# Latent attention scores with 288 rows of contraction as two full matmuls and one of 32 rows, the 32-row ones for four blocks on four row sets of the array

## The chip, the cores and the metric

The kernel runs on 1 core of one Trainium2 chip. The metric is the device time in microseconds (us). The kernel before takes 2636.1 us, the median of 3 runs (2635.48 to 2636.65).

## The reference

One layer of a transformer trunk over 1024 latent tokens and 256 context tokens, D = 1024: a SwiGLU half step, two attention branches side by side (2-D neighbourhood attention, "NA", and multi-head latent attention, "MLA"), a gated merge, and a second SwiGLU half step. The change lies in the MLA scores. Cut to that:

```python
def _mla_k(k_nope, k_rope):                 # 64 own dims of a head, 32 rope dims shared by all heads
    return jnp.concatenate([k_nope, broadcast(k_rope)], axis=-1)

def _attend(q, k, v):                       # 8 heads, q 96 wide, keys: 256 context + 1024 latent
    s = jnp.einsum('bqhd,bkhd->bhqk', q * q.shape[-1] ** -0.5, k)
    p = jax.nn.softmax(s, axis=-1)
    return jnp.einsum('bhqk,bkhd->bqhd', p, v)
```

## The kernel before

Every float32 operand of a product is held as a high and a low part, and a product is made of three matmuls: high by high, high by low, low by high (`mm3`). For a score the contraction is 96 rows (64 own, 32 rope), so three matmuls of 96 rows stand for 288 rows of contraction, each with 32 rows of the array empty.

The attention stage runs 64 items: 32 of NA, then 32 of MLA. An MLA item is one head and 256 queries (two sets s of 128). `MlaItem.scores` makes, for each s, two score blocks of 512 latent keys (e = 0, 1) and one of 256 context keys, each in a PSUM bank; `copy_max` (L1639, VectorE) copies a block to SBUF and leaves its row maximum; L1771 (VectorE) reduces these to one maximum per row; L1775 (ScalarE) takes the exponentials, two long ones of 1024 keys and two short ones of 256, in the order long, short, long, short of the program. `MlaItem.values` works in five parts p0 to p4 of 256 keys: four transposes on TensorE into a bank of pool "m", a high part cast out of it on ScalarE (L1801), a low part by a subtraction on VectorE (L1802), and two parts later four 256-column matmuls on these (`w` below). `head_out` (L1611 to L1620) ends an item: one 64-row copy on ScalarE (L1615) in one item, three (L1611, L1612, L1615) in the next, and an addition on VectorE (L1616); every second item has two more transposes (L156, rope). "One-copy" and "three-copy" items alternate.

The main loop runs the scores of item n+3 beside the values of item n: before, a fifth of the scores (one `yield`) goes behind the transposes of each part. TensorE keeps its order as written. The other engines' operations in these functions are placed by a scheduler; each engine runs its own in order. PSUM has 3 banks of pool "s", 3 of "m", 2 of "v", each pool used in turn. The latent-token and context parts of q, k and v come from DRAM scratch by DMAs that one queue (SP) issues; `MlaHead` issues 14 of them for a head, when the first item of that head is started. Tiles of pool "w" (16) hold them, 6 for a head.

Of the kernel before, what the change touches and what calls it, by code (L numbers as in the profile page):

```python
# [9 lines left out]
F32R = mybir.dt.float32r  # L10
# [5 lines left out]
P = 128  # L16
# [3 lines left out]
NLAT = 1024  # L20
NCTX = 256
# [3 lines left out]
QK = 96  # L25
# [13 lines left out]
def f32(ap):  # L39
    return ap.bitcast(F32)  # L40
# [3 lines left out]
def hybrid_block(ctx: ExitStack, tc: tile.TileContext, a: dict, out: bass.AP):  # L44
# [22 lines left out]
    def U(dt=F32, key="u"):  # L67
        return pools[key].tile([P, 1024], dt, tag="u", name=nm("x" + key))
# [4 lines left out]
    def W(dt=F32R):  # L73
        return pools["w"].tile([P, 1024], dt, tag="w", name=nm("w"))
# [13 lines left out]
    def PB(tag):  # L88
        return ps.tile([P, 512], F32, tag=tag, name=nm("b" + tag), bufs=PBUFS[tag])
# [22 lines left out]
    class Engine:  # L112


        def __init__(self, e):
            self.e = e
# [5 lines left out]
    def ld(dst, src):  # L122
        for x in [x for x in waiting if x[1].tensor.name == src.tensor.name]:
            waiting.remove(x)
            put(*x[1:])
        return put(dst, src)
# [23 lines left out]
    vec, act, pool = Engine(nc.vector), Engine(nc.scalar), Engine(nc.gpsimd)  # L150

    def mmul(o, s, m, start, stop):
        return pin(nc.tensor.matmul(o, s, m, start=start, stop=stop, skip_group_check=open_group[0]))  # L153
# [4 lines left out]
    def mm3(o, s, m, start, stop):  # L158
        mmul(o, s[0], m[0], start=start, stop=False)
        mmul(o, s[0], m[1], start=False, stop=False)  # L160
        mmul(o, s[1], m[0], start=False, stop=stop)
# [182 lines left out]
    cols = {}  # L344
# [618 lines left out]
    o = len(plan.main)  # L963
# [7 lines left out]
    e = len(plan.main)  # L971
# [50 lines left out]
    o = len(plan.main)  # L1022
# [6 lines left out]
    for i, d in enumerate(downs):  # L1029
        last = i == len(downs) - 1  # L1030
        o = len(plan.main)
# [535 lines left out]
    o = va_at  # L1567
# [70 lines left out]
    def copy_max(dst, src, m):  # L1638
        nc.vector.tensor_scalar(dst, src, 1.0, FMIN, op0=ALU.mult, op1=ALU.max, accum_out=m)  # L1639
# [90 lines left out]
            return [local, context, edge]  # L1730

    class MlaHead:
        def __init__(self, h):
            self.h = h
            self.qh, self.ql, self.kh, self.kl, self.v, self.kvc = [W() for _ in range(6)]
            b, i = (h % 2) * 64, (h % 4) * 32
            for s, x in enumerate((self.qh, self.ql)):
                ld(f32(x[0:64, :]), qns[h // 2][s, b:b + 64, :])
                ld(f32(x[64:QK, :]), qrs[h // 4][s, i:i + 32, :])
                ld(f32(self.kvc[0:64, s * 256:(s + 1) * 256]), kns[h // 2][s, b:b + 64, NLAT:])  # L1740
                ld(f32(self.kvc[64:QK, s * 256:(s + 1) * 256]), krs[s, :, NLAT:])
            for s, x in enumerate((self.kh, self.kl)):
                ld(f32(x[0:64, :]), kns[h // 2][s, b:b + 64, :NLAT])
                ld(f32(x[64:QK, :]), krs[s, :, :NLAT])
            vsv = vs[:, h * P:(h + 1) * P].rearrange("(t p) c -> p t c", p=P)
            ld(f32(self.v).rearrange("p (t c) -> p t c", t=8), vsv[:, 0:8, :])
            ld(f32(self.kvc[:, 512:768]).rearrange("p (t c) -> p t c", t=2), vsv[:, 8:10, :])

    class MlaItem:
# [2 lines left out]

        def scores(self):
            hd, b = self.head, self.b
            cx = PB("s")
            m, n_, l, r = ST(8), ST(2), ST(4), sums_of(self.n)
            self.prl, self.prc = prl, prc = [U(), U()], T2()
            qq = [[x[:QK, b * 256 + s * P:b * 256 + (s + 1) * P] for x in (hd.qh, hd.ql)] for s in range(2)]
            for s in range(2):
                mm3(cx[:, s * 256:(s + 1) * 256], qq[s], [hd.kvc[:QK, 0:256], hd.kvc[:QK, 256:512]], True, True)  # L1760
            for s in range(2):
                copy_max(prc[:, s * 256:(s + 1) * 256], cx[:, s * 256:(s + 1) * 256], m[:, 3 * s + 2:3 * s + 3])
            yield
            for s in range(2):
                for e in range(2):
                    lat = PB("s")
                    mm3(lat, qq[s], [x[:QK, e * 512:(e + 1) * 512] for x in (hd.kh, hd.kl)], True, True)
                    copy_max(prl[s][:, e * 512:(e + 1) * 512], lat, m[:, 3 * s + e:3 * s + e + 1])
                    if s + e < 2:
                        yield  # L1770
            nc.vector.tensor_reduce(n_, m[:, 0:6].rearrange("p (s c) -> p s c", s=2), axis=AX.X, op=ALU.max, negate=True)  # L1771

            def exp(x, i):
                s = i % 2
                nc.scalar.activation(x, x, AF.Exp, bias=n_[:, s:s + 1], accum_out=l[:, i:i + 1])  # L1775

            def total():
                nc.vector.tensor_tensor(r, l[:, 0:2], l[:, 2:4], op=ALU.add)
                nc.vector.reciprocal(r, r)
                if self.n % 2:  # L1780
                    widen(self.n)

            for s in range(2):
                soft.append(lambda s=s: exp(prl[s], s))
                soft.append(lambda s=s: exp(prc[:, s * 256:(s + 1) * 256], 2 + s))
            soft.append(total)
            yield
# [411 lines left out]
```

## Time and profile before

| What | Value |
|---|---|
| Median of 3 runs | 2636.1 us |
| Profiled execution, its own time / span | 2633.94 us / 2632.2 us |
| TensorE (PE) busy | 2602.1 us, 99% |
| TensorE weight loads (PEld) busy | 2215.3 us, 84% |
| VectorE (DVE) busy | 1854.2 us, 70% |
| ScalarE (ACT) busy | 1151.8 us, 44% |
| Chain that ended last | PE 56%, issue 32%, DVE 5%, ACT 5% |
| Granted TensorE clock | 0.999 of full speed |

The shares are means over stages with different limits. A busy TensorE is not TensorE at its peak: matmuls are pipelined, so the records of neighbours overlap, and what a matmul costs is the distance from its start to the next one's start. The MLA items lie between about 1495 and 1770 us. In the rows below, "[1.18 <-DVE st L1771]" means that the engine sat idle for 1.18 us before the instruction and that VectorE's line 1771 ended it.

### The profile page before, as it was taken

To read this page: it belongs to the slowest core of one execution; us is meant where nothing else is said; L and a number is where in the kernel's file an instruction comes from. 1 tells how busy PE (TensorE), PEld (TensorE's weight loads), DVE (VectorE), ACT (ScalarE), POOL (GpSimd) and SP (SyncE) were. 2 spreads that over 40 slices of the span, in tenths; PEclk is the share of its full clock that TensorE was granted. 3 is DMA by queue.
4 is the path that set the end of the run, shared out by engine and by line. 5 is a ranking of instruction groups with operands and counts; after the bars stand their busy time and mean duration, and the time that the engine had idled before them with its cause. 6 is when DMAs were issued, how large, how long until landed. Compare 5 with 4: busy or idle time off the path is not lost.

```text
span 2632.2 us, 37730 instructions
## 1 busy us (share of the span) xinstructions
PE 2602.1 (99%) x13728; PEld 2215.3 (84%) x13728; DVE 1854.2 (70%) x3478; ACT 1151.8 (44%) x2193; POOL 220.3 (8%) x368
## 2 busy tenths in 40 slices
PE   8999999999999999999999999999999999999998
PEld 6888888888888788889889999987888888888887
DVE  4778876588776676864569988877436777565876
ACT  6622223522223753433439887772365222234111
POOL 1000000000000400001004422220020000000001
PEclk9999999999999999999999999999999999999999
DMA  8544433444433665745977723217244433225333
GB/s 303 166 157 145 150 106 125 157 160 161 163 130 99 229 227 188 247 150 181 304 285 281 211 75 75 67 49 230 86 148 166 138 120 109 76 92 193 120 96 128
DMA packets 196218, 414.14 MB, mean 157 GB/s; under 512 B 24960, under 2 KB 66112, under 8 KB 196032
## 3 DMA queue, kind: packets, MB, share of 16 engines
q1 hardware_dynamic: 196032, 411.73, 47.3%
q8 instruction: 108, 1.77, 0.3%
q14 instruction: 78, 0.64, 0.1%
HBM read 308.30 MB, written 103.35 MB: 156 GB/s over the span
## 4 chain that ended last, share of the span: by engine, by line
PE 56%; issue 32%; DVE 5%; ACT 5%; DMA 1%; POOL 1%; SPq 0%; DVEq 0%; POOLq 0%; ACTq 0%
PE bs L153 23%; PE bm L153 17%; PE bv L153 13%; PE bm L156 2%; ACT xu L1775 1%; DVE xu L1639 1%; DVE t L1802 1%; ACT t L1801 1%; DVE xv L120 1%; PE bs L156 1%; POOL st L120 1%; ACT t L120 1%; DVE t L120 1%; DVE xu L120 1%; ACT t L1775 0%
## 5 line engine op out<-in xcount | busy, mean ns | idle before, releaser
L153 PE MATMUL bm<-xu,xu 128*128 128x512 f32 (+2 forms) x2376 | 569.4, 388 | 0.9 <-ACT t L120 0.6
L153 PEld LDWEIGHTS bm<-xu,xu 128*128 128x128 f32 x2376 | 437.5, 188 | 89.9 <-ACT t L120 1.9
L153 PE MATMUL bs<-xu,xu 128*128 128x512 f32 (+1 forms) x1800 | 433.5, 385 | 0.0
L153 PEld LDWEIGHTS bs<-xu,xu 128*128 128x128 f32 x1800 | 332.3, 188 | 67.4 <-issue 0.8
L153 PE MATMUL bs<-xv,xu 128*128 128x512 f32 x1488 | 357.3, 389 | 0.3 <-DVE t L120 0.3
L153 PE MATMUL bv<-xv,xu 128*128 128x512 f32 x1342 | 335.4, 389 | 0.0
L153 PEld LDWEIGHTS bs<-xv,xu 128*128 128x128 f32 x1488 | 279.2, 188 | 58.6 <-issue 0.7
L120 ACT CAST xu<-t 128x512 fp32r<-128x512 f32 x260 | 158.2, 616 | 355.8 <-DVE t L120 354.6
L153 PEld LDWEIGHTS bv<-xv,xu 128*128 128x128 f32 x1342 | 251.9, 188 | 52.3
L120 DVE TENSOR_TENSOR xu<-t,xu 128x512 fp32r<-128x512 f32 x260 | 178.5, 688 | 127.2 <-ACT xu L120 127.2
L120 DVE TENSOR_TENSOR xu<-xv,xu 128x512 fp32r<-128x512 f32 (+2 forms) x244 | 182.3, 767 | 57.1 <-ACT xu L120 54.0
L153 PE MATMUL bs<-w,w 96*128 96x512 f32 (+3 forms) x832 | 206.2, 366 | 2.5 <-DVE st L1664 2.2
L120 POOL TENSOR_SCALAR st<-st 128x1 f32<-128x1 f32 (+1 forms) x66 | 34.6, 524 | 1977.8 <-ACT t L120 1959.4
L120 DVE TENSOR_TENSOR xu<-xu,xu 128x512 fp32r<-128x512 f32 (+1 forms) x218 | 151.0, 698 | 67.1 <-ACT xu L120 66.7
L120 ACT CAST xu<-xv 128x512 fp32r<-128x512 f32 (+2 forms) x216 | 136.8, 692 | 125.9 <-DVE xv L120 60.3
L153 PE MATMUL bm<-t,xu 128*128 128x256 f32 (+1 forms) x1272 | 165.3, 287 | 0.6 <-ACT t L120 0.4
L153 PEld LDWEIGHTS bm<-t,xu 128*128 128x128 f32 x1272 | 160.7, 191 | 6.0 <-ACT t L120 0.8
L153 PE MATMUL bv<-xu,xu 128*128 128x512 f32 x602 | 161.7, 389 | 0.0
L120 ACT ACTIVATE t<-t 128x512 f32<-128x512 f32 (+1 forms) x94 | 57.3, 609 | 221.6 <-DVE t L120 212.6
L153 PE MATMUL bv<-t,w 128*128 128x256 f32 x896 | 151.5, 288 | 2.7 <-DVE t L1802 2.0
L153 PEld LDWEIGHTS bv<-t,w 128*128 128x128 f32 x896 | 132.8, 189 | 18.5 <-DVE t L1802 6.8
L120 ACT CAST xu<-xu 128x512 fp32r<-128x512 f32 (+1 forms) x218 | 134.2, 627 | 15.8 <-DMA xu<-in_f1w 8.1
(216 smaller groups left out, 3679.2 us busy)
## 6 DMA issues: line engine op xcount, KB each, us to landing
d<-t SPq DMA_DIRECT2D x272, 256.0 KB, 2.8
xv<-d SPq DMA_DIRECT2D x68, 512.0 KB, 4.5
xv<-in_f1w SPq DMA_DIRECT2D x64, 512.0 KB, 3.6
xu<-in_f1w SPq DMA_DIRECT2D x61, 512.0 KB, 3.8
xu<-in_f2w SPq DMA_DIRECT2D x60, 512.0 KB, 3.8
t<-in_wada SPq DMA_DIRECT2D x112, 256.0 KB, 3.9
t<-d SPq DMA_DIRECT2D x76, 256.0 KB, 3.3
xu<-in_winT SPq DMA_DIRECT2D x38, 512.0 KB, 4.6
```

What stands on the lines that cost most here:

```text
L120: return lambda *x, **y: pin(f(*x, **y))
L153: return pin(nc.tensor.matmul(o, s, m, start=start, stop=stop, skip_group_check=open_group[0]))
L156: return pin(nc.tensor.transpose(o, x, i))
L1639: nc.vector.tensor_scalar(dst, src, 1.0, FMIN, op0=ALU.mult, op1=ALU.max, accum_out=m)
L1775: nc.scalar.activation(x, x, AF.Exp, bias=n_[:, s:s + 1], accum_out=l[:, i:i + 1])
L1801: nc.scalar.copy(t[0], pb)
L1802: nc.vector.tensor_tensor(t[1], pb, f32(t[0]), op=ALU.subtract)
```

## The change

The 288 rows of contraction are laid out anew. `q1` (128 rows) holds q high (64), rope high (32) and rope low (32); `k1` holds k high (64), rope high (32) and rope high again. `q2` holds q high and q low; `k2` holds k low and k high. So two matmuls of 128 rows do 256 of the 288 rows. What is left, rope high of q by rope low of k, has 32 rows. `q3` and `k3` hold these for the four latent blocks on four sets of 32 partitions, and four 32-row matmuls, one for each block and each on its own rows of the array, open the four blocks' banks together at the head of an item. For the context block the third product is a 128-row matmul against `c3`, zero but for 32 rows.

The latent blocks now come first in an item and the context block last; of the four latent banks the first comes from pool "m" and three from "s", and the context bank from "m". `MlaHead` issues 21 loads for a head, and 5 once for a tile of pool "y" that all heads share (`k3`, `c3`), which two memsets on GpSimd clear in part. A head takes 7 tiles of pool "w".

```diff
     class MlaHead:
+        shared = None
         def __init__(self, h):
-            self.qh, self.ql, self.kh, self.kl, self.v, self.kvc = [W() for _ in range(6)]
+            self.q1, self.q2, self.q3, self.k1, self.k2, self.v, self.kvc = [W() for _ in range(7)]
             b, i = (h % 2) * 64, (h % 4) * 32
-            for s, x in enumerate((self.qh, self.ql)):
-                ld(f32(x[0:64, :]), qns[h // 2][s, b:b + 64, :])
-                ld(f32(x[64:QK, :]), qrs[h // 4][s, i:i + 32, :])
-                ld(f32(self.kvc[0:64, s * 256:(s + 1) * 256]), kns[h // 2][s, b:b + 64, NLAT:])
-                ld(f32(self.kvc[64:QK, s * 256:(s + 1) * 256]), krs[s, :, NLAT:])
-            for s, x in enumerate((self.kh, self.kl)):
-                ld(f32(x[0:64, :]), kns[h // 2][s, b:b + 64, :NLAT])
-                ld(f32(x[64:QK, :]), krs[s, :, :NLAT])
+            if MlaHead.shared is None:
+                x = MlaHead.shared = U(F32R, "y")
+                for p in ((0, 64), (96, P)):
+                    pool.memset(f32(x[p[0]:p[1], 512:512 + NCTX]), 0.0)
+                ld(f32(x[64:QK, 512:512 + NCTX]), krs[1, :, NLAT:])
+                for g in range(4):
+                    ld(f32(x[32 * g:32 * g + 32, 0:512]), krs[1, :, (g % 2) * 512:(g % 2) * 512 + 512])
+            self.k3, self.c3 = MlaHead.shared[:, 0:512], MlaHead.shared[:, 512:512 + NCTX]
+            q, r, n = qns[h // 2], qrs[h // 4], kns[h // 2]
+            parts = [(self.q1, [(0, q[0, b:b + 64, :]), (64, r[0, i:i + 32, :]), (QK, r[1, i:i + 32, :])]),
+                     (self.q2, [(s * 64, q[s, b:b + 64, :]) for s in range(2)])]
+            for k, o, c in ((self.kvc, 0, slice(NLAT, NLAT + NCTX)), (self.k1, None, slice(0, NLAT))):
+                one = k[:, 0:NCTX] if o == 0 else k
+                two = k[:, NCTX:2 * NCTX] if o == 0 else self.k2
+                parts += [(one, [(0, n[0, b:b + 64, c]), (64, krs[0, :, c]), (QK, krs[0, :, c])]),
+                          (two, [(64 - s * 64, n[s, b:b + 64, c]) for s in range(2)])]
+            for x, rows in parts:
+                for o, y in rows:
+                    ld(f32(x[o:o + y.shape[0], :]), y)
+            for g in range(4):
+                ld(f32(self.q3[32 * g:32 * g + 32, 0:512]).rearrange("p (b c) -> p b c", b=4),
+                   r[0, i:i + 32, :].rearrange("p (b s c) -> p b s c", b=4, s=2)[:, :, g // 2, :])
...
         def scores(self):
-            cx = PB("s")
...
-            qq = [[x[:QK, b * 256 + s * P:b * 256 + (s + 1) * P] for x in (hd.qh, hd.ql)] for s in range(2)]
+            pairs = [(s, e) for s in range(2) for e in range(2)]
+            lats = [PB("m" if x == 0 else "s") for x in range(4)]
+            for g, lat in enumerate(lats):
+                rows = slice(32 * g, 32 * g + 32)
+                mmul(lat, hd.q3[rows, b * P:(b + 1) * P], hd.k3[rows, :], True, False)
+            cols = [slice(b * 256 + s * P, b * 256 + (s + 1) * P) for s in range(2)]
+            for (s, e), lat in zip(pairs, lats):
+                keys = slice(e * 512, (e + 1) * 512)
+                mmul(lat, hd.q1[:, cols[s]], hd.k1[:, keys], False, False)
+                mmul(lat, hd.q2[:, cols[s]], hd.k2[:, keys], False, True)
+                copy_max(prl[s][:, keys], lat, m[:, 3 * s + e:3 * s + e + 1])
+                yield
+            cx = PB("m")
             for s in range(2):
-                mm3(cx[:, s * 256:(s + 1) * 256], qq[s], [hd.kvc[:QK, 0:256], hd.kvc[:QK, 256:512]], True, True)
+                x = cx[:, s * 256:(s + 1) * 256]
+                mmul(x, hd.q1[:, cols[s]], hd.kvc[:, 0:256], True, False)
+                mmul(x, hd.q2[:, cols[s]], hd.kvc[:, 256:512], False, False)
+                mmul(x, hd.q1[:, cols[s]], hd.c3, False, True)
             for s in range(2):
                 copy_max(prc[:, s * 256:(s + 1) * 256], cx[:, s * 256:(s + 1) * 256], m[:, 3 * s + 2:3 * s + 3])
-            yield
-            for s in range(2):
-                for e in range(2):
-                    lat = PB("s")
-                    mm3(lat, qq[s], [x[:QK, e * 512:(e + 1) * 512] for x in (hd.kh, hd.kl)], True, True)
-                    copy_max(prl[s][:, e * 512:(e + 1) * 512], lat, m[:, 3 * s + e:3 * s + e + 1])
-                    if s + e < 2:
-                        yield
             nc.vector.tensor_reduce(n_, m[:, 0:6].rearrange("p (s c) -> p s c", s=2), axis=AX.X, op=ALU.max, negate=True)
```

The scheduler also places VectorE's and ScalarE's work differently. VectorE before, at the end of a three-copy item (subtractions of p3 and p4, the last score block `xu`, the maximum, then p0 of the next item; `bm` and `bs` are PSUM banks):

```order
L1802 TENSOR_TENSOR t_16074<-bm_16068,t_16073 128x512
L1778 TENSOR_TENSOR st_15767<-st_15887 128x2
L1802 TENSOR_TENSOR t_16093<-bm_16087,t_16092 128x512
L1779 RECIPROCAL st_15767<-st_15767 128x2
L1639 TENSOR_SCALAR xu_16004,st_15999<-bs_16099 128x512
L1771 TENSOR_REDUCE st_16000<-st_15999 128x2
L1802 TENSOR_TENSOR t_16115<-bm_16109,t_16114 128x512
```

VectorE of the change at the same place (L1830 is L1802, L1799 is L1771):

```order
L1830 TENSOR_TENSOR t_17598<-bm_17592,t_17597 128x512
L1806 TENSOR_TENSOR st_17292<-st_17412 128x2
L1830 TENSOR_TENSOR t_17615<-bm_17609,t_17614 128x512
L1807 RECIPROCAL st_17292<-st_17292 128x2
L1639 TENSOR_SCALAR t_17530,st_17524<-bm_17621 128x256 x2
L1830 TENSOR_TENSOR t_17641<-bm_17635,t_17640 128x512
L1799 TENSOR_REDUCE st_17525<-st_17524 128x2
L1639 TENSOR_SCALAR xu_17648,st_17645<-bm_17651 128x512
L1639 TENSOR_SCALAR xu_17648,st_17645<-bs_17652 128x512
```

The two context copies have taken the place of a latent one, and the subtraction of the next p0 now stands ahead of the maximum instead of behind it; two latent copies follow the maximum at once.

ScalarE before, in a three-copy item from its first long exponential on (`128x1024` the long ones, `128x256` the short ones, `t<-bm` the casts of p1 to p4):

```order
L1775 ACTIVATE xu_15888,st_15887<-xu_15888,st_15886 128x1024
L1801 CAST t_16023<-bm_16018 128x512
L1775 ACTIVATE t_15890,st_15887<-t_15890,st_15886 128x256
L1775 ACTIVATE xu_15889,st_15887<-xu_15889,st_15886 128x1024
L1611 COPY t_16037<-bv_15943 64x256
L1612 COPY t_16040<-bv_15943 64x256
L1615 COPY t_16037<-bv_15943 64x256
L1801 CAST t_16053<-bm_16048 128x512
L1775 ACTIVATE t_15890,st_15887<-t_15890,st_15886 128x256
L1801 CAST t_16073<-bm_16068 128x512
L1801 CAST t_16092<-bm_16087 128x512
```

ScalarE of the change at the same place (L1803 is L1775, L1829 is L1801):

```order
L1803 ACTIVATE xu_17413,st_17412<-xu_17413,st_17411 128x1024
L1829 CAST t_17551<-bm_17546 128x512
L1803 ACTIVATE t_17415,st_17412<-t_17415,st_17411 128x256
L1611 COPY t_17563<-bv_17467 64x256
L1612 COPY t_17566<-bv_17467 64x256
L1615 COPY t_17563<-bv_17467 64x256
L1829 CAST t_17579<-bm_17574 128x512
L1803 ACTIVATE xu_17414,st_17412<-xu_17414,st_17411 128x1024
L1829 CAST t_17597<-bm_17592 128x512
L1803 ACTIVATE t_17415,st_17412<-t_17415,st_17411 128x256
L1829 CAST t_17614<-bm_17609 128x512
```

The second long exponential has moved from ahead of the copies to behind the cast of p2, so it stands ahead of the cast of p3.

## Rows read from the trace of the kernel before

**Rows 1.** Stages: start:end us, length, busy us (instructions) by engine, clock, DMA.
```profile
1557.31:1565.95 8.64, 8.59 (x62) 7.78 (x61) 7.06 (x22) 7.09 (x17) 2.26 (x4) 1.00 0.56 136
1524.06:1750.08 226.02, 225.03 (x1599) 207.47 (x1598) 190.89 (x568) 180.20 (x406) 55.74 (x95) 1.00 0.23 58
```

**Rows 2.** Timeline, ScalarE, a three-copy and a one-copy item: start us, duration us, instruction.
```profile
1591.04 1.15 ACT L1775 ACTIVATE xu<-xu,st 128x1024 f32<-128x1024 f32 x1 [1.18 <-DVE st L1771]
...
1592.18 0.56 ACT L1801 CAST t<-bm 128x512 fp32r<-128x512 f32 x1
1592.65 0.51 ACT L1775 ACTIVATE t<-t,st 128x256 f32<-128x256 f32 x1
...
1593.15 1.15 ACT L1775 ACTIVATE xu<-xu,st 128x1024 f32<-128x1024 f32 x1
...
1594.29 0.36 ACT L1611 COPY t<-bv 64x256 f32<-64x256 f32 x1
...
1594.93 0.37 ACT L1615 COPY t<-bv 64x256 f32<-64x256 f32 x1
1595.32 0.59 ACT L1801 CAST t<-bm 128x512 fp32r<-128x512 f32 x1
...
1599.44 1.16 ACT L1775 ACTIVATE xu<-xu,st 128x1024 f32<-128x1024 f32 x1 [1.07 <-DVE st L1771]
...
1602.60 0.19 ACT L1775 ACTIVATION_READ_ACCUMULATOR xu<-xu,st 128x1 f32 x1
1602.82 0.37 ACT L1615 COPY t<-bv 64x256 f32<-64x256 f32 x1
...
1607.67 1.16 ACT L1775 ACTIVATE xu<-xu,st 128x1024 f32<-128x1024 f32 x1 [1.15 <-DVE st L1771]
```

**Rows 3.** Timeline, VectorE, the same three-copy item.
```profile
1591.52 0.41 DVE L1639 TENSOR_SCALAR_CACHE_REDUCE t<-bs 128x256 f32<-128x256 f32 x1
...
1591.86 0.42 DVE L1639 TENSOR_SCALAR_CACHE_REDUCE t<-bs 128x256 f32<-128x256 f32 x1
...
1592.78 0.69 DVE L1802 TENSOR_TENSOR t<-bm,t 128x512 fp32r<-128x512 f32 x1 [0.50 <-ACT t L1801]
1593.39 0.68 DVE L1639 TENSOR_SCALAR_CACHE_REDUCE xu<-bs 128x512 f32<-128x512 f32 x1
...
1595.33 0.41 DVE L1616 TENSOR_TENSOR t<-t,bv 64x256 f32<-64x256 f32 x1 [0.64 <-ACT t L1615]
1595.94 0.69 DVE L1802 TENSOR_TENSOR t<-bm,t 128x512 fp32r<-128x512 f32 x1 [0.20 <-ACT t L1801]
...
1599.25 0.16 DVE L1771 TENSOR_REDUCE st<-st 128x2 f32<-128x6 f32 x1
```

**Rows 4.** Timeline, TensorE, the same item: first start us, us to last end, instructions merged.
```profile
1588.93 0.95 PE L153 MATMUL bs<-w,w 96*128 96x256 f32 x6
1589.72 0.64 PE L153 MATMUL bv<-t,w 128*128 128x256 f32 x4
1590.20 0.60 PE L156 MATMUL bm<-ident,xu 128*128 128x128 f32 x4
1590.55 0.94 PE L153 MATMUL bs<-w,w 96*128 96x512 f32 x3
1591.33 0.64 PE L153 MATMUL bv<-t,w 128*128 128x256 f32 x4
1591.81 0.38 PE L156 MATMUL bv<-ident,rope 128*128 128x128 f32 x2
```

**Rows 5.** Timeline, TensorE, eight 32-column matmuls on four column sets, and what follows.
```profile
1847.42 0.64 PE L153 MATMUL bv<-t,strip 128*32 128x256 f32 x8
1847.99 1.20 PE L153 MATMUL bm<-xo,xu 128*128 128x512 f32 x4
```

**Rows 6.** Timeline, SP: DMA issues for the first two MLA heads, merged.
```profile
1477.45 22.72 SPq L132 DMA_DIRECT2D w<-d  x30
```

**Rows 7.** Timeline, TensorE, the first MLA scores.
```profile
1495.54 0.84 PE L153 MATMUL bs<-w,w 96*128 96x256 f32 x5
```

## The prediction, made before the changed kernel ran

> **What bounds the kernel now.** I read the page first: TensorE is busy 99% of the span and heads the chain that ended last, which says that every matmul taken away is time won. So the second view is the stages, for the MLA items alone: in 226.02 us from 1524 to 1750 TensorE has 225.03 busy, but VectorE 190.89 and ScalarE 180.20 [rows 1]. These are 27 items (a long exponential starts each), 8.37 us an item, of which VectorE has 7.07 to do. The third view is the timelines of one item, engine by engine, and it turns the picture round.
>
> ScalarE waits over a microsecond for VectorE's maximum before the first long exponential of every item (1.18, 1.07, 1.15), and VectorE then waits for ScalarE: for the cast of p1 behind that exponential (0.50), for the copy L1615 (0.64), for the cast of p2 (0.20) [rows 2, 3]. No wait on TensorE stands among VectorE's. Follow a three-copy item from its exponential at 1591.04: long exponential, cast, short, long exponential, three copies, cast of p2 at 1595.32, all end to end on ScalarE; 0.62 later the subtraction of p2 at 1595.94; from there VectorE works without a gap to the maximum at 1599.25, and 0.19 later the next exponential starts, at 1599.44 [rows 2, 3]. That is a closed loop of 8.40 us over two engines, without TensorE. The one-copy item behind it takes 8.23, to 1607.67 [rows 2], so a pair takes 16.63. Every second head has 8.64 in place of 8.40 [rows 1].
>
> What would TensorE alone need? By distances of starts [rows 4]: four transposes 0.35 (1590.20 to 1590.55), three 512-column matmuls 0.78 (to 1591.33), four 256-column ones 0.48 (to 1591.81), the six context matmuls 0.79 (1588.93 to 1589.72). A part with a latent block is 1.61, the one with the context block 1.62: 8.06 an item, and some 0.2 for the two rope transposes in every second one (half of 0.35), so 16.3 a pair against 16.63 measured. TensorE is a close second, busy since its records overlap, and it is the loop that sets the pace.
>
> **The change part by part.**
>
> *TensorE's matmuls.* An item loses twelve 512-column matmuls of 0.26 (a third of 0.78) and gets eight, and four of 32 rows. If these run beside each other they cost about one. No row shows row sets; the nearest one is of column sets: eight 256-column matmuls on four sets, two rounds, take 0.57 from the first start to the next full matmul (1847.42 to 1847.99), where four full ones of that width already take 0.48 [rows 4, 5]. That holds the change to another layout of the array and back. So the four cost from 0.26 (one matmul) through 0.57 (the eight) to 1.04 (four times 0.26, no overlap). I take 0.35, nearer to the packed end. TensorE then needs 0.35 + 0.35 + 0.52 + 0.48 = 1.70 for the first part, 1.35 for each of the next three, 1.62 for the last: 7.37 an item, 0.69 less than 8.06, and 15.0 a pair. Taken at its word that is 32 x 0.69 = 22 us, the gain if TensorE set the pace. In the last part 0.48 and 0.79 are as before: the context block keeps six matmuls.
>
> The Trainium skill (TensorEngine Tiling (Array Packing), Key Properties) says that a change of tiling mode drains TensorE. No row separates such a drain; one lies inside the 0.57 of [rows 5], so the trace neither contradicts it nor prices it. The same page (PSUM Bottleneck) warns that packing speeds TensorE but not the emptying of PSUM; that is this loop, on which the trace decides.
>
> *VectorE and ScalarE.* No operation is added or removed in an item: five casts, five subtractions, four latent copies, two context copies, one maximum, four exponentials. Their places change, as the pieces of order show. Two moves matter. The subtraction of the next p0 now runs ahead of the maximum (0.61 more on the loop there: 1592.78 to 1593.39 [rows 3]) and two latent copies follow the maximum at once, where VectorE used to have a subtraction and two context copies. And the second long exponential stands behind the cast of p2: p2 comes out of ScalarE 1.15 earlier, p3 later.
>
> So I walk the loop again, with the distances of [rows 2, 3]: long exponential to next 1.14, cast to short exponential 0.47, short to next 0.50, first copy to third 0.64, third copy to cast 0.39, cast to subtraction 0.60, L1615 to L1616 0.40, a subtraction or latent copy on VectorE 0.61, a context copy 0.34 (1591.52 to 1591.86), maximum to exponential 0.19. I take 0.07 for each of the small reciprocal and sum.
>
> Three-copy item, exponential at 0. ScalarE: cast p1 1.14, short 1.61, copies from 2.11 to 2.75, cast p2 3.14, long 3.61, cast p3 4.75, short 5.22, cast p4 5.72. VectorE: two copies from -0.11, done at 1.11; subtraction p1 1.74 (waits for its cast); copy 2.35; L1616 3.15 (waits); p2 3.74 (waits); copy 4.35; p3 5.35 (waits); p4 6.32 (waits); sum and reciprocal; context copies 7.07 and 7.41; p0 7.75; maximum 8.36; exponential 8.55.
>
> One-copy item. The copy starts 0.22 behind a readout (1602.60 to 1602.82), here at 2.24; cast p2 2.63, long 3.10, cast p3 4.24, short 4.71, cast p4 5.21. VectorE: p1 1.74; L1616 2.64; p2 3.23; copies 3.84 and 4.45; p3 5.06; p4 5.81 (waits); context copies from 6.56; p0 7.31; maximum 7.92; exponential 8.11.
>
> The pair: 16.66 against 16.63. Waits have moved from one operation to another, and the loop is as long as before. The 8.64 of every second head stays, since ScalarE's copies stand on the path in both walks. Each start in the walk may be off by some 0.1 an item: 16 pairs at 0.03, bounds -3 and +4 us; I take +0.5.
>
> *What is late next.* The first latent bank now comes from pool "m", where three banks pass in turn through seven uses an item. It gets the bank that p4 has just left, so the four 32-row matmuls wait for the subtraction of p4 (6.32 + 0.69 = 7.01 in the three-copy item), and all of TensorE's queue behind them: the four latent blocks, the transposes of p1 and on to the next p0. TensorE needs some 7.4 from there to the end of the next p0's transposes, at 7.01 + 7.4 - 8.55 = 5.9 of the next item; its cast must have started by 6.7 for the subtraction at 7.31. About 0.8 of slack by these rows, less by pipeline tails of 0.2 to 0.4 (a record's 0.94 against 0.78, [rows 4]) after each wait. So TensorE's time won turns into a wait of its own for p4, and costs nothing as long as the 32-row matmuls are packed.
>
> *Loads.* A head takes 21 loads for 14, the first one 26 with the shared tile. SP issued 30 in 22.72 us, 0.76 each, waits for free buffers among them [rows 6]. For later heads SP has an item's time and more to spare: hidden. For the first, 14 x 0.76 ended at 1488, and 26 x 0.76 end at 1497, where the first scores stood at 1495.54 [rows 7]; the 32-row operands come near the end. TensorE may stall once, from 0 to some 5 us with landing; the last three NA items lie ahead and part of it hides there. I take 1. The two memsets lie on GpSimd ahead of these loads: nothing.
>
> *Sum.* The profiled execution has 2633.94 us of its own (span 2632.2): +0.5 + 1 = 2635.4. The runs' median is 2.2 above the profiled one, so I predict 2637.6, rounded to 2637.5.
>
> **The rivals.**
>
> *TensorE sets the pace after all.* For it: 99% busy, and VectorE's 7.07 an item leave room below 8.3. Against: VectorE's waits are all on ScalarE, and the loop closes without TensorE. If the loop gave way fully: 22 us, 2614; half of it, if the new order of the two engines is shorter than my walk: 2625. I name 2624.
>
> *The 32-row matmuls run one after another, or the layout change is dear.* For it: no row of row sets. Against: the column sets of [rows 5]. They cost 1.04, TensorE needs 16.3 a pair again, and now with the wait for p4 in its queue: the 0.8 of slack less tails is gone, and 0.3 to 0.9 a pair come on top, 16 x 0.6 = 10 us: 2646, slower. It decides from about 0.8 us for the four. Behind it stands the Trainium skill (TensorE: Matmul & The Clock Gate, Part 3), which gives 3.07 times for four row tiles: by that the four would cost 0.34 (an estimate: 4 x 0.26 / 3.07), which is the packed case; no run here shows it yet.
>
> *The first loads stall more, and the loop is longer by 0.2 a pair*: 3 + 3 us, 2643.
>
> **How the numbers follow.** The forecast 0.60 (its own range 2632 to 2643), TensorE's pace 0.15, unpacked 0.14, loads and a longer loop 0.11. Within 0.2% is 2630.8 to 2641.4, about what a measurement of this kernel can tell from no change. Faster: 0.13 of the first rival and 0.02 of the forecast, 0.15. Slower: 0.14, most of 0.11 and 0.03 of the forecast, 0.26. Same: 0.59. The range for 8 in 10 leaves out most of the first rival and half of the second: 2629 to 2646.
>
> **What would show it.** Right: an MLA item still 8.2 to 8.4 us from exponential to exponential; ScalarE still waiting for the maximum; TensorE idle some 0.5 an item, in front of the 32-row matmuls with VectorE's L1830 as the releaser; the four of them starting within a few ns of each other. Wrong: items of 7.5 to 8.0 us; or the four starting 0.2 us apart; or TensorE waiting for a DMA at 1495 for more than 3 us.

## The result and the profile after

| | Before | Changed |
|---|---|---|
| Median (lowest to highest), 20 runs of each | 2635.98 us (2633.22 to 2637.91) | 2640.18 us (2637.03 to 2643.34) |
| Ratio to before, 95% interval | | 1.0016 (1.0009 to 1.0022) |
| Span of the profiled execution | 2632.2 us | 2635.3 us |
| TensorE busy in it | 2602.1 us | 2596.0 us |
| 27 steady MLA items | 226.02 us | 226.03 us |

The change is 4 us slower, by the interval 0.09 to 0.22%, which is about the 0.2% that the prediction calls no change. TensorE's saving bought nothing in the steady items, and something was lost elsewhere. The windows of the changed kernel show both (columns as in [rows 1]); the first stretch is the entry, from the transposes ahead of the first MLA scores to the exponential that opens the 27 items.

```profile
1493.50:1526.72 33.22, 29.55 (x204) 25.28 (x203) 27.50 (x90) 23.54 (x56) 11.08 (x20) 1.00 0.76 179
...
1526.72:1752.75 226.03, 219.18 (x1595) 192.90 (x1594) 191.30 (x568) 179.88 (x406) 55.90 (x95) 1.00 0.36 81
```

The same view of the kernel before, for the entry from the same point of the program on:

```profile
1494.60:1524.06 29.46, 29.32 (x206) 26.87 (x205) 26.72 (x89) 23.51 (x55) 10.61 (x18) 1.00 0.50 123
```

The entry is 3.76 us longer with TensorE no busier (29.55 against 29.32): 3.67 us in which it stood idle, against 0.14. The 27 items answer to the second of [rows 1]: as long as before, TensorE busy 5.85 us less, VectorE and ScalarE as before. So nothing was hidden by chance: the saving turned into idle time.

The two spans differ by only 3.1 us, because the changed kernel reaches the entry 1.10 us earlier (1493.50 for 1494.60), in a stretch that the change doesn't touch. From the entry to the end it loses 4.2 us: 3.76 in the entry, 0.01 in the 27 items, some 0.4 behind them. There TensorE waits once for 1.24 us for a cast on ScalarE, until 1764.40 (the longest such wait before is 0.45), and its granted clock is 0.74 from 1764 to 1768.

**A steady item.** ScalarE's timeline, the changed kernel (start, duration, instruction, idle time before it and who ended it):

```profile
1593.68 1.15 ACT L1803 ACTIVATE xu<-xu,st 128x1024 f32<-128x1024 f32 x1 [0.95 <-DVE st L1799]
...
1602.19 1.15 ACT L1803 ACTIVATE xu<-xu,st 128x1024 f32<-128x1024 f32 x1 [0.95 <-DVE st L1799]
...
1610.32 1.15 ACT L1803 ACTIVATE xu<-xu,st 128x1024 f32<-128x1024 f32 x1 [0.97 <-DVE st L1799]
```

These answer to [rows 2]: 8.51 and 8.13 from exponential to exponential, 16.64 a pair, where before had 8.40 and 8.23, 16.63. ScalarE still waits for the maximum (L1799 is L1771). VectorE closes the loop as in [rows 3]:

```profile
1594.80 0.69 DVE L1639 TENSOR_SCALAR_CACHE_REDUCE xu<-bs 128x512 f32<-128x512 f32 x1 [0.55 <-PE bs L153]
...
1600.05 0.69 DVE L1830 TENSOR_TENSOR t<-bm,t 128x512 fp32r<-128x512 f32 x1 [0.22 <-ACT t L1829]
...
1601.40 0.68 DVE L1830 TENSOR_TENSOR t<-bm,t 128x512 fp32r<-128x512 f32 x1
1602.01 0.15 DVE L1799 TENSOR_REDUCE st<-st 128x2 f32<-128x6 f32 x1
```

p4 waits for its cast, then the context copies, p0 and the maximum follow without a gap, and the exponential comes 0.18 behind it. Waits of VectorE for TensorE are new: 0.55 for the second latent block here and 0.28 for the third, 19.4 us in 41 waits over the 27 items, where the same view of the kernel before lists none. They take the place of waits for ScalarE (for casts 10.6 us in place of 22.4, for L1615 1.0 in place of 10.3). They are absorbed: the subtraction of p2 starts when its cast lets it, and the maximum comes 8.33 behind the exponential, where the prediction's walk has 8.36. TensorE in the same item (answering to [rows 4]):

```profile
1600.79 0.49 PE L153 MATMUL bm<-xy,w 32*128 32x512 f32 x1 [0.25 <-DVE t L1830]
1600.80 0.50 PE L153 MATMUL bs<-xy,w 32*128 32x512 f32 x3
```

The four start within 10 ns, so they do run beside each other, and they wait for the subtraction of p4 (L1830), which ends at 1600.74.

**The entry.** TensorE's timeline, the changed kernel:

```profile
1494.06 0.60 PE L156 MATMUL bm<-ident,xu 128*128 128x128 f32 x4
1495.69 0.46 PE L153 MATMUL bm<-xy,w 32*128 32x512 f32 x1 [1.03 <-DVE st L1671]
1495.86 1.17 PE L153 MATMUL bs<-xy,w 32*128 32x512 f32 x3
1496.96 0.73 PE L153 MATMUL bm<-w,w 128*128 128x512 f32 x2
...
1509.38 0.47 PE L153 MATMUL bm<-xy,w 32*128 32x512 f32 x1 [0.86 <-DVE xu L1699]
...
1517.16 0.46 PE L153 MATMUL bm<-xy,w 32*128 32x512 f32 x1 [1.78 <-DVE st L1807]
```

Three stalls, each in front of 32-row matmuls: 1.03, 0.86 and 1.78 us, together the 3.67 us of idle time. The second and third are for a PSUM bank that VectorE has not yet left: the subtraction L1699 that empties it ends at 1509.22 and at 1517.01 (the third names the reciprocal just behind it). The first names an instruction of VectorE, but it is for operands: the four loads of `q3`, issued from 1491.05 to 1492.99, land at 1495.60, 1495.82, 1496.10 and 1496.43, and the four matmuls start one by one just behind, at 1495.69, 1495.86, 1496.19 and 1496.56. From the transposes to the first full matmul 2.90 us pass, 0.97 where nothing waits. The queue, SP's timeline, says why:

```profile
1475.80 0.42 SPq L132 DMA_DIRECT2D xy<-in_bias  x1
1479.08 2.17 SPq L132 DMA_DIRECT2D xy<-d  x5
1481.35 21.07 SPq L132 DMA_DIRECT2D w<-d  x32
```

SP stands 2.9 us before the shared tile's loads (`xy<-d`), whose buffer an NA bias tile still holds, and `q3` comes last of the operands in the loads behind them.

### The profile page after: what moved, and what is told of

It reads as the page before. It is cut to its first block, busy times and chain, and to the rows that moved or that the text cites. A ratio compares the mean times of both kernels' runs of the same rounds, so it can differ in the third digit from the quotient of the medians.

```text
span 2635.3 us, 37805 instructions
## 1 busy us (share of the span) xinstructions
PE 2596.0 (99%) x13728; PEld 2200.2 (83%) x13728; DVE 1854.6 (70%) x3478; ACT 1151.7 (44%) x2193; POOL 220.7 (8%) x370
## 3 DMA queue, kind: packets, MB, share of 16 engines
q8 instruction: 108, 1.77, 0.3%
## 4 chain that ended last, share of the span: by engine, by line
PE 54%; issue 32%; ACT 7%; DVE 5%; POOL 1%; DMA 1%; SPq 0%; DVEq 0%; POOLq 0%; ACTq 0%
PE bs L153 22%; PE bm L153 17%; PE bv L153 12%; ACT xu L1803 2%; ACT t L1829 2%; PE bm L156 2%; DVE xv L120 1%; DVE t L1830 1%; POOL st L120 1%; PE bs L156 1%; ACT t L1803 1%; DVE t L120 1%; DVE xu L120 1%; DVE t L1639 1%; ACT t L120 1%
## 5 line engine op out<-in xcount | busy, mean ns | idle before, releaser
L153 PEld LDWEIGHTS bv<-xu,xu 128*128 128x128 f32 x602 | 112.7, 188 | 23.2
```

## The experiments

My theory, 1: VectorE and ScalarE set the pace of the steady items through the maximum, TensorE's saving becomes waiting, and the 4 us are lost at the entry. The rivals: TensorE sets the pace and the layout change eats its saving; or the loss is spread over all items.

**e_late_before, e_late_after, e_pin_after: is it the loop?** An exponential is issued one item later, so it never waits for a fresh maximum. The same edit is made on both kernels, and ScalarE's instructions of these items are pinned in the order of the program (`pin(...)` around them, not shown). In the changed kernel that is the order that ScalarE has anyway, and the third run, with the pins alone, is the control. In the kernel before it is not: the pins also move the second long exponential from ahead of the copies ([rows 2]) to behind the cast of p2, where the change has it, and no run has the pins alone on that kernel. So the exponentials are not "in the same places" there, as the first expectation has it. VectorE's order is the scheduler's in all three; with late exponentials one latent copy of a three-copy item changes places with the addition L1616.

```diff
+    late = []
...
         soft_n, soft[:] = list(soft), []
+        if n + 2 >= 4 * NH:
+            late.append(soft_n)
+            soft_n = late.pop(0) if len(late) > 1 else []
```

> The kernel before, with the exponentials of an MLA item issued one item later (two items after its scores, still one item ahead of their use), in the same places of ScalarE's order, which is pinned. No exponential waits for a maximum that has just been made. Theory 1 (the loop of VectorE and ScalarE through the maximum sets the pace, 16.63 a pair, and TensorE alone would need 16.3 to 16.4): the wait for the maximum goes, items take 8.15 to 8.2, 3 to 5 us less than before, 2631 to 2633. Rival (TensorE or VectorE's own work sets the pace): no change, 2636.

> The change, with the exponentials of an MLA item issued one item later, as in the run on the kernel before. Theory 1 (the loop hides TensorE's gain): with the loop through the maximum open, TensorE's own need shows, 7.4 to 7.6 us an item, and the way from the cast of p1 over the subtraction of p4 and the 32-row matmuls to the next cast of p1 takes some 7.5; 8 to 20 us less than the change, 2620 to 2632, and far more than the same edit gives the kernel before. Rival 1 (TensorE's saving is eaten by the layout change, TensorE sets the pace): no change, 2640. Rival 2 (VectorE's order alone sets it): as much as the same edit gives the kernel before, about 2636.

> The change with ScalarE's casts, copies and exponentials of the MLA items pinned in the order of the program, and nothing else: the control for the runs with late exponentials, which pin them too. Theory 1 (it is the age of the exponentials, not the pinned order, that opened the loop): as the change, 2639 to 2641, items 8.5 and 8.1 in turn. Rival (the pinned order itself gave the gain): 2630 to 2633.

Measured: 2632.65 us (0.9987, 0.9978 to 0.9996), 2631.48 (0.9986, 0.9977 to 0.9994), and the control 2641.29 (1.0021, 1.0012 to 1.0030), with its 8.51 and 8.12 unchanged. ScalarE in e_late_before, where the pins have moved the second long exponential:

```profile
1595.16 0.59 ACT L1801 CAST t<-bm 128x512 fp32r<-128x512 f32 x1
1595.64 1.15 ACT L1775 ACTIVATE xu<-xu,st 128x1024 f32<-128x1024 f32 x1
```

Windows over the same 27 items; first the kernel before with late exponentials:

```profile
1525.89:1747.58 221.69, 221.69 (x1596) 207.35 (x1595) 197.17 (x568) 181.14 (x408) 55.44 (x94) 1.00 0.24 60
```

then the changed one:

```profile
1525.16:1743.36 218.20, 215.05 (x1594) 192.60 (x1594) 189.96 (x566) 181.64 (x408) 55.77 (x95) 1.00 0.38 85
```

With the loop open the kernel before is held by TensorE: busy 221.69 of 221.69, pairs of 16.41, close to the 16.3 that the prediction adds up from starts. The items had taken 4.3 us more (3.3 by the medians); how much of that is the later exponential and how much the moved one isn't shown. The changed kernel gains 7.8 in the same items, 8.7 by the medians, and there the control leaves only the age of the exponentials and that one exchange on VectorE: theory 1, and both rivals fall. But the gain is at the small end of 8 to 20, since TensorE's own need was wrong. Side by side, with late exponentials in both, the change is 3.5 us shorter in the 27 items but only 1.2 by the medians, within their scatter: at its entry TensorE still waits 1.38, 0.59 and 0.65 us in front of 32-row matmuls.

**e_serial, e_lazy: what do the four 32-row matmuls cost?** All four on row set 0, then each alone in front of its block's pair.

```diff
 e_serial
-                rows = slice(32 * g, 32 * g + 32)
+                rows = slice(0, 32)
...
 e_lazy
+                if apart:
+                    lats[g] = PB("s")
+                    rope_rows(g)
+                lat = lats[g]
                 mmul(lat, hd.q1[:, cols[s]], hd.k1[:, keys], False, False)
```

> The change, but all four 32-row matmuls read rows 0 to 31 (of q3 and k3), so that they follow one another on one row set; two of the four blocks then get another block's keys or queries for their last 32 rows. In the trace of the change the four start within 10 ns and the path from the last transpose to the first full matmul is some 0.6 us longer than without them. Theory 1 (they run beside each other, and TensorE has under 0.5 us an item to spare behind the loop of VectorE and ScalarE): the four start some 0.2 us apart, 0.6 to 0.8 more an item, TensorE needs 8.5 to 8.7 and becomes the bound: 2645 to 2652. Rival (what the four cost is the layout change, not their work, or the records only look parallel): no change, 2640.

> The change, but each of the four 32-row matmuls stands alone, directly in front of the two full matmuls of its block, on its own row set, and all four banks come from pool s. Four changes of the array's layout an item in place of one. Theory 1 (the price of the four, some 0.6 us on TensorE's path, is nearly all the change of layout and back, paid once for four): each costs 0.5 to 0.6, TensorE needs some 9.5 us an item, 1.2 to 1.5 above the loop: 2670 to 2684. Rival (the layout change is free and a 32-row matmul costs what a full one does, 0.24): TensorE needs 8.2, and with the waits for pool m gone at the entry 2636 to 2641.

Measured: 2648.67 us (1.0052, 1.0039 to 1.0066; four runs) and 2683.9 (1.0184, 1.0165 to 1.0202; two runs). In e_serial the 27 items take 235.95 us, 9.9 more than in the change, so it is the steady items that pay. One part of an item on TensorE, from its transposes to the next ones. The kernel before (late exponentials), three matmuls of 96 rows, 1.61:

```profile
1616.79 0.60 PE L156 MATMUL bm<-ident,xu 128*128 128x128 f32 x4
1617.14 0.94 PE L153 MATMUL bs<-w,w 96*128 96x512 f32 x3
...
1618.40 0.60 PE L156 MATMUL bm<-ident,xu 128*128 128x128 f32 x4
```

The change (late exponentials), a part without 32-row matmuls, 1.37, and one with the four, unhindered, 2.01:

```profile
1615.19 0.60 PE L156 MATMUL bm<-ident,xu 128*128 128x128 f32 x4
1615.54 0.70 PE L153 MATMUL bs<-w,w 128*128 128x512 f32 x2
...
1616.56 0.60 PE L156 MATMUL bm<-ident,xu 128*128 128x128 f32 x4
...
1620.95 0.60 PE L156 MATMUL bm<-ident,xu 128*128 128x128 f32 x4
1621.48 0.50 PE L153 MATMUL bm<-xy,w 32*128 32x512 f32 x1
1621.48 0.50 PE L153 MATMUL bs<-xy,w 32*128 32x512 f32 x3
1621.92 0.73 PE L153 MATMUL bm<-w,w 128*128 128x512 f32 x2
...
1622.96 0.38 PE L156 MATMUL bm<-ident,xu 128*128 128x128 f32 x2
```

e_lazy, one 32-row matmul alone, 1.99:

```profile
1600.09 0.60 PE L156 MATMUL bm<-ident,xu 128*128 128x128 f32 x4
1600.62 0.50 PE L153 MATMUL bs<-xy,w 32*128 32x512 f32 x1
1601.04 0.72 PE L153 MATMUL bs<-w,w 128*128 128x512 f32 x2
...
1602.08 0.38 PE L156 MATMUL bm<-ident,xu 128*128 128x128 f32 x2
```

e_serial, four on one row set:

```profile
1600.56 0.49 PE L153 MATMUL bm<-xy,w 32*128 32x512 f32 x1
1600.90 0.85 PE L153 MATMUL bs<-xy,w 32*128 32x512 f32 x3
1601.68 0.73 PE L153 MATMUL bm<-w,w 128*128 128x512 f32 x2
```

A full matmul costs 0.24 (1.61 less 1.37). One 32-row matmul alone costs 0.62 (1.99 less 1.37), four beside each other 0.64, four on one row set 0.68 more (1.12 to the first full matmul for 0.44), 1.32. So some 0.4 (0.62 less 0.24) is the way into the other layout and back, paid once a group. The weight loads, which elsewhere run ahead, show it in the changed kernel (late exponentials):

```profile
1621.48 0.18 PEld L153 LDWEIGHTS bm<-xy,w 32*128 32x128 f32 x1 [0.17 <-DVE st L1806]
...
1621.91 0.30 PEld L153 LDWEIGHTS bm<-w,w 128*128 128x128 f32 x2 [0.24 <-DMA w<-d]
```

0.17 of idle going in, 0.24 coming out; e_lazy has the same 0.17 and 0.25. The releasers named are not the cause, as they differ from group to group. In e_lazy TensorE sets the pace (busy in all 257.61 us of 1531.39 to 1789.00, items of 9.65 and 9.74), and its second and third MLA item do not wait for a bank at the entry. It takes one bank at a time, and all from pool "s", and TensorE is slower in it; which of these spares it the wait isn't shown.

**e_loads, e_entry: the entry.** The four loads of `q3` first and the shared tile late; then the first three MLA items one part later.

```diff
 e_loads
...
+            for g in range(4):
+                ld(f32(self.q3[32 * g:32 * g + 32, 0:512]).rearrange("p (b c) -> p b c", b=4),
...
+            rows_in(first + parts[:2])
             if MlaHead.shared is None:
...
+            rows_in(parts[2:])
...
 e_entry
+            if self.n < 4 * NH + 3:
+                yield
             lats = [PB("m" if x == 0 else "s") for x in range(4)]
```

> The change with the loads of a head in another order: the four of q3 first, then q1, q2, k1 and k2, and only then the shared tile and the context parts, so that the queue no longer waits for the shared tile's buffer ahead of everything. Theory 1 (the four us are lost at the entry into the MLA items, some 2 of them because the 32-row operands come last in the queue): the wait in front of the first four 32-row matmuls, 1.03 us and the spread of the other three, is gone and the time falls by 1.5 to 2, to 2638 to 2639. Rival (the entry loses its time to the banks alone): no change, 2640.

> The change, but the first three MLA items, whose scores run beside NA items of three parts, begin one part later. Their 32-row matmuls then take the bank that the context block has left, in place of the one that the part just before has left. Theory 1 (two stalls of 1.1 and 2.0 us for that bank, and part of a third for the loads): 3 to 4.5 us less than the change, 2635.5 to 2637. Rival (the loss is spread over all the items, as the cost of the layout change or a longer loop): 2639 to 2640.

Measured: 2640.88 us (1.0018, 1.0010 to 1.0027) and 2638.84 (1.0013, 1.0004 to 1.0021). Both gave less than theory 1 asked. TensorE's timeline in e_loads:

```profile
1497.19 0.60 PE L156 MATMUL bm<-ident,xu 128*128 128x128 f32 x4
...
1497.73 0.51 PE L153 MATMUL bs<-xy,w 32*128 32x512 f32 x2
1498.44 0.49 PE L153 MATMUL bs<-xy,w 32*128 32x512 f32 x1 [0.20 <-DVE xu L1639]
1498.86 0.74 PE L153 MATMUL bm<-w,w 128*128 128x512 f32 x2
```

The wait for loads is gone, and behind it a wait of the fourth for an "s" bank appears: a second bank wait that the late loads had covered. 1.2 of 1.9 us are won there (1.67 from transposes to the first full matmul, for 2.90), and lost again in this execution at 1520 (below). The medians show no gain. Sorted by the mean granted clock of a run they hint at one: eight of the eleven runs of e_loads are at 0.997 and take 2640.38 to 2641.34 us, the change's four at 0.997 take 2642.91 to 2643.34. So the loads may be worth some 2 us, spent again where the clock fell more often; that isn't shown. In e_entry stalls of 0.45, 0.52 and 1.12 us are left, of 3.67 before: VectorE leaves other banks late too, once in front of transposes. The intervals of its ratio and of the change's overlap, so its 1.3 us is not shown; that the entry holds the loss is shown by the windows, not by these two.

**v_first3, v_all, v_two, v_two_vec: what can be had.** Late exponentials, the loads of e_loads, and the 32-row matmuls later in the item: in the first three items by one part; in all by one; in all others by two; and the last with VectorE pinned in program order too.

```diff
+            for _ in range(1 if self.n < 4 * NH + 3 else 2):
+                yield
             lats = [PB("m" if x == 0 else "s") for x in range(4)]
```

> The change with the exponentials one item later, the first three MLA items begun one part later, and the loads of a head in the order q3, q1, q2, k1, k2, shared tile, context. The sum of three edits measured alone (8.7, 1.3 and no gain by the medians; in the traces 1.4 of the entry's 3.8 us and 1.1 of the first stall). Theory 1: 2629 to 2630.5, all three beside each other. Rival (the entry's stalls only move, since VectorE is late there): 2631.5, as with the late exponentials alone.

> As the run before it in this list, but every MLA item begins one part later, behind the transposes of p1, so that its first latent bank is the one that the context block has left and not the one of p4. With the loop open the trace of the change shows items of 8.0 to 8.25 where TensorE's own start distances add to 7.8 and 7.9 with rope: 0.2 to 0.4 a pair is the wait of the 32-row matmuls on the subtraction of p4. Theory 1: this wait goes, pairs of 15.8 to 15.9 in place of 16.1 to 16.25: 4 to 6 us less than the run before it, 2624 to 2626. Rival (VectorE's own chain sets these items, or the wait comes back on the context block's bank): no gain, 2629 to 2631.

> As the run in which every MLA item begins one part later, but two parts later (one for the first three items): the 32-row matmuls stand behind the transposes of p2, and the bank of pool m that they take is that of p0, which VectorE has left long before, not that of the context block, for which they still wait 0.34 a pair. Theory 1: no wait in front of them, pairs of 15.75 to 15.85 in place of 16.1, which is what TensorE's start distances add to: 3 to 5 us less, 2624 to 2626. Rival (with 7.07 of 7.9 us busy VectorE sets the items, and the three blocks now bunched in the last part make another wait): 2628 to 2632.

> As the run before it in this list, with VectorE's work of the MLA items pinned in the order of the program too, so that no copy of a block stands in front of a subtraction whose operands are there earlier. Theory 1: as the run before it or up to 2 us less, 2623 to 2626. Rival (the maximum and the copies in program order make VectorE late, as it waits for each in turn): 2628 to 2634.

Measured: 2629.78 us (0.9978, 0.9968 to 0.9987), 2629.07 (0.9977, 0.9968 to 0.9986), 2628.64 (0.9976, 0.9967 to 0.9986), 2632.8 (0.9989, 0.9980 to 0.9998). The first three beat both kernels, by 6 to 7 us before and by 10 to 12 the change; among themselves they can't be told apart. But the late exponentials alone bring the kernel before to 2632.65, so what the new layout of the scores, with its entry mended, adds to that is 2.9 to 4.0 us by the medians. v_first3 came out as the sum of its edits, one of which (1.3) wasn't clear of noise by itself. v_all did not bring 4 to 6 us more: the wait moved to the bank of the context block, in TensorE's timeline of v_all:

```profile
1615.66 0.50 PE L153 MATMUL bm<-xy,w 32*128 32x512 f32 x1 [0.27 <-DVE t L1639]
```

v_two frees TensorE almost wholly:

```profile
1526.13:1742.38 216.25, 215.26 (x1597) 192.41 (x1596) 190.11 (x566) 177.13 (x407) 55.60 (x94) 1.00 0.38 86
```

Busy 215.26 of 216.25, pairs of 15.90 (16.13 in every second head), and 1.9 us less than in v_first3 (218.14), but by the medians only 1.1 of it reaches the end, within the scatter. Behind the items, in the matmuls on the attention's output (`xo`), TensorE in v_two has a wait for ScalarE that it does not have in v_first3:

```profile
1775.59 3.30 PE L153 MATMUL bs<-xo,xu 128*128 128x512 f32 x12 [1.33 <-ACT xu L120]
```

v_two_vec shows that VectorE's order matters by 4 us: in program order its addition L1616 waits 12.5 us for ScalarE's copies between 1535 and 1740, in v_two 2.6, while its waits for casts fall from 16.9 to 12.9.

## Why the prediction was right, and where it was not

*The sum.* It adds 0.5 for the loop and 1 for the entry; measured are 0.0, 3.8, and 0.4 behind the items. So the forecast of no change came true by the mechanism that it named, and the 2.7 us that it missed (2640.2 for 2637.5) are at the entry.

*The loop.* Right, and to 0.04 us: 8.55 and 8.11 walked, 8.51 and 8.11 to 8.13 measured; the pair 16.66 against 16.63. Of a three-copy item the walk's starts hold within 0.1 from p2 on; before it, two latent copies and L1616 come 0.2 to 0.6 later than walked, behind the waits for TensorE that the walk did not have. The term of +0.5 for 32 items is +0.01 for 27. In every second head the three-copy item became 8.74, not 8.64, and the item behind it 8.11, not 8.22: the pair stayed. The sign of "still 8.2 to 8.4" holds for the mean of 8.37, not for single items, as the walk itself had said. e_late_after with its control e_pin_after shows the loop as cause, which the prediction had only argued.

*The four 32-row matmuls at 0.35.* Mis-sized: 0.64, inside the bounds of 0.26 to 1.04 but beyond the 0.57 of [rows 5]. The upper bound itself was too low: four on one row set cost 1.32, as 1.04 had left out the layout change. TensorE's need is 2.01 + 3 x 1.37 + 1.64 (the last part's is as before) = 7.76 an item, not 7.37, and the saving 0.32, not 0.69. So TensorE is idle 0.25 an item (6.85 us in 27), not some 0.5. It cost nothing in the time, since the loop hides the saving either way. But it corrects the first rival: opened fully, the change could give 10 us, not 22. By the two late runs 3.5 came in 27 items, by v_two 5.4.

The Trainium skill (TensorEngine Tiling (Array Packing), Key Properties) says that a change of mode drains TensorE; the trace agrees now, and prices it: 0.62 for a matmul that is worth 0.24. The Trainium skill (TensorE: Matmul & The Clock Gate, Part 3) gives 3.07 times for four row tiles; this kernel's path shows another figure: 0.64 for 1.32 on one row set, 2.1 times, and 0.24 for 0.92, 3.8 times, when the 0.4 for the change of layout is taken off both (an estimate).

*The wait for the bank of pool "m", which "costs nothing as long as the 32-row matmuls are packed".* True for the steady items: weight loads and matmuls wait there for L1830 and the items are no longer. It failed at the entry, and this is the step that cost most. The prediction worked out the slack for an item of five parts. Beside an NA item of three parts it is likewise the bank of the last part that comes round, but there VectorE has two latent copies and L1616 to do first and leaves it 0.9 and 1.8 us too late. No loop was there to hide it, as TensorE was the bound in that stretch: before, it was busy for 29.32 of 29.46 us, and by the distances of starts only 0.4 of these were not its own work.

*The first loads at 1.* They cost up to 1.9 in the profiled execution, with a bank wait beneath. The queue issued them faster than at 0.76 each (24 in 14.6 us, up to the last of `q3`). What was overlooked is the 2.9 us that it stood before the shared tile's buffer, ahead of all loads, and that those of `q3` land 3.4 to 4.6 us behind their issue. The two memsets ran behind these loads, at 1497.6 and 1497.9, and not ahead of them; no wait shows for it.

*The rivals.* TensorE's pace: false, as e_late_after and e_pin_after show. Unpacked: they are packed; e_serial, which unpacks them, came out 8.5 above the change, as the rival had said of it (2646 against 2637.5). Loads and a longer loop: half true; loads and banks at the entry, no longer loop.

## What to carry to other kernels

Work taken off the busiest engine pays only where that engine ends the waits: follow the waits round one period before counting, and to open such a loop let the consumer work on older data (one item of age here, without a buffer more) and then count again. A group on row sets pays its change of layout once, so it must replace at least three full matmuls to be worth it here (0.64 against 0.24 each); and it needs all its banks at one moment, so look who leaves each of them last, in the first and last items too and not only in the steady ones.

## What was not expected of the hardware

TensorE's granted clock falls after single stalls, and not in every execution. v_two, the window behind a wait of 1.87 us for VectorE that ends at 1383.68, in a stretch that no edit touches (the granted clock is the third number from the end):

```profile
1383.68 2.22 PE L153 MATMUL bs<-w,w 128*128 128x256 f32 x8 [1.87 <-DVE st L1664]
...
1384.00:1388.00 4.00, 4.00 (x19) 3.75 (x18) 3.08 (x17) 0.37 (x1) 0.00 (x0) 0.57 0.91 316
```

The kernel before, behind the same wait of 1.87 us, which ends at 1382.29:

```profile
1382.29 1.79 PE L153 MATMUL bs<-w,w 128*128 128x256 f32 x8 [1.87 <-DVE st L1664]
...
1384.00:1388.00 4.00, 4.00 (x36) 4.00 (x34) 3.85 (x18) 3.12 (x8) 0.00 (x0) 1.00 0.98 358
```

Here the clock stayed at 2.4 GHz; in v_two it went down towards 1.2, and its lag behind the kernel before, instruction by instruction on ScalarE, grew from 1.4 to 2.8 us across this place. All thirteen traces have this wait, of 1.87 or 1.88 us; in nine the granted clock is 0.57 to 0.61 over the 4 us behind it, in four (before, the change, e_late_after, e_lazy) 1.00. In e_loads it fell behind the entry's third stall, of 1.77 us, behind which the change's own profiled execution (1.78 us) kept 1.00:

```profile
1520.00:1524.00 4.00, 4.00 (x21) 3.71 (x19) 1.63 (x7) 3.44 (x7) 1.02 (x2) 0.58 0.30 82
```

So a stall can cost nearly twice its length (1.87 us and 1.4 more in v_two), and the scatter between runs goes with it: of the change's 20 runs the seven with a mean clock of 0.999 or more took 2637.0 to 2639.0 us, the nine at 0.998 2639.6 to 2642.0, the four at 0.997 2642.9 to 2643.3. A stall that a change adds is paid for nearly twice in some of them.
